# Attention scores in 64-row halves of the array: queries split on 128 rows, three passes for each head

## The chip, the cores and the metric

The kernel runs on one core of a Trainium2 chip. The metric is the device time in microseconds from the first to the last instruction on that core. The kernel before takes 1592.31 us (median of three runs, 1591.7 to 1594.3).

## What is computed

The reference is a two-layer encoder over 512 tokens of width 1024. Each layer norms its input, projects it, runs a state-space branch and an attention branch, projects both back, adds the residual, and then runs a gated feed-forward block. Cut to the part that matters here (16 query heads of 64 channels, 4 key heads, blocks of 128 queries that see the 128 keys before and behind):

```python
def one_block(args):
    qb, n = args
    kb = lax.dynamic_slice_in_dim(kp, start, KEY_SPAN, axis=1)
    vb = lax.dynamic_slice_in_dim(vp, start, KEY_SPAN, axis=1)
    s = jnp.einsum("bqgrd,bkgd->bgrqk", qb, kb,
                   preferred_element_type=jnp.float32) * scale + bias
    s = jnp.where(valid, s, -jnp.inf)
    m = jnp.maximum(jnp.max(s, axis=-1, keepdims=True), sink_l)
    p = jnp.exp(s - m)
    denom = jnp.sum(p, axis=-1, keepdims=True) + jnp.exp(sink_l - m)
    return jnp.einsum("bgrqk,bkgd->bqgrd", (p / denom).astype(vb.dtype), vb)
```

## The kernel before, in words

Matrices in float32 are split into a leading part and a trailing part (`hi`, `lo`, both of type fp32r), and a product is made of three matmuls, hi by hi, hi by lo and lo by hi. `mm3` (L263 to L265) issues these three for all dense projections; they write to the four PSUM banks of `dense_bank` (printed as `pd`). Each matmul is preceded by a load of its stationary operand (LDWEIGHTS, printed as PEld).

The attention of a layer lies beside dense work. `g_q` makes the query projection of a head group (4 heads), and its `done` takes the two result banks (two heads each, 64 rows a head) and makes four query tiles: ScalarE writes the scaled leading part on the head's own 64 rows (L629), VectorE the trailing part on the other 64 rows (L630). `k_done` has put the leading part of the keys on both halves of 128 rows (`kst_h`), and the trailing part likewise (`kst_l`). So one matmul of 128 rows takes leading and trailing queries against the leading keys, and a second one takes them against the trailing keys:

```python
mm(ps[:, :w], q, kst_h[:, g, it.k0 : it.k0 + w], start=True, stop=False)
mm(ps[:, :w], q, kst_l[:, g, it.k0 : it.k0 + w], start=False, stop=True)
```

`attn_scores` does this (L557, L558) for each of the four heads of an item, an item being one block of 128 queries of one group: w is 256 keys for the first and the last block of the sequence and 384 for the two between them. That is 2 layers x 4 groups x 4 blocks x 4 heads = 128 heads, 64 at each width. VectorE then adds the bias and takes the maximum (L559), which frees the head's bank. Score banks, transposes and value products share the four banks of `small_bank` (printed as `psm`). `attn_turn` transposes the softmax (L591; ScalarE copies the bank out in L593), `attn_values` multiplies by the values (L601) with the two halves of the columns of the array, 64 columns each, and `attn_push` runs values, turn and scores of three successive items in a row.

The `Side` object spreads these items between the steps of the dense projections, and a scheduler then sets the final order of the instructions on each engine from its own priorities. So where the score matmuls stand among the dense ones is read from the built program, not from the code.

Of the kernel before, what the change touches and what calls it, by code (L numbers as in the profile page):

```python
# [14 lines left out]
P = 128  # L15
L = 512
# [33 lines left out]
def encoder_kernel(  # L50
# [27 lines left out]
    def f(ap):  # L78
        return ap.bitcast(F32)
# [16 lines left out]
    def nm(s):  # L96
        uid[0] += 1
        return f"{s}_{uid[0]}"
# [4 lines left out]
    def small_bank():  # L103
        return pss.tile([P, 512], F32, tag="s", name=nm("psm"))

    # ------------------------------------------------------------------
    # weights: raw float32 units, split into a leading and a trailing part
    # ------------------------------------------------------------------
    units = []
# [13 lines left out]
    def kcols(w, kt0, nkt, c0, ncol):  # L123
        """rows kt0*128.. of w, columns c0..c0+ncol, as [p, kt, col]"""
        return w[kt0 * P : (kt0 + nkt) * P, c0 : c0 + ncol].rearrange("(k p) c -> p k c", p=P)
# [9 lines left out]

    # a unit is (key, [(kt0, nkt, col0, ncols, offset, pitch)], matrix)
    def prep_raw(n):
# [56 lines left out]

    # ------------------------------------------------------------------
    # constants
    # ------------------------------------------------------------------
    def tri(name, op, base, cm, step, src):
# [47 lines left out]
    def load_toep(g):  # L246
        """the table rows of a head group, once for each query of a block"""
        src = table[4 * g : 4 * g + 4].unsqueeze(0).broadcast_to([P, 4, 512])
        nc.gpsimd.dma_start(toep[g].rearrange("h p c -> p h c"), src)
# [8 lines left out]

    # ------------------------------------------------------------------
    # helpers  # L260
    # ------------------------------------------------------------------
    def mm3(o, lh, ll, rh, rl, start, stop):
# [14 lines left out]
    def norm_token(npool, t, wb, dst):  # L277
        """RMS norm of token tile t, transposed and split into dst = [(hi, lo)] * 2"""
        xn = npool.tile([P, D], F32, tag="xn", name=nm("xn"), bufs=4)
        ss = smp.tile([P, 2], F32, tag="ss", name=nm("ss"))  # L280
        halves = [slice(512 * b, 512 * b + 512) for b in range(2)]
        for b, cs in enumerate(halves):
            sq = xn[:, cs]
            if dst is None and b == 0:
                G.tensor_tensor(sq, x_sb[t][:, cs], wb[:, cs], ALU.mult)
                sq = npool.tile([P, 512], F32, tag="sq", name=nm("sq"), bufs=2)
            S.activation(sq, x_sb[t][:, cs], AF.Square, scale=1.0 / 32.0, accum_out=ss[:, b : b + 1])  # L287
        rs = smp.tile([P, 1], F32, tag="rs1", name=nm("rs"))
        G.tensor_scalar(rs, ss[:, 0:1], ss[:, 1:2], EPS, ALU.add, ALU.add)  # L289
        G.tensor_tensor(rs, rs, mhalf, ALU.pow)  # L290
        for b, cs in enumerate(halves):
            if dst is None:
                if b == 0:
                    S.mul(xn[:, cs], xn[:, cs], rs)
                else:
                    V.scalar_tensor_tensor(xn[:, cs], x_sb[t][:, cs], rs, wb[:, cs], ALU.mult, ALU.mult)
                nc.sync.dma_start(out[t * P : (t + 1) * P, cs], xn[:, cs])
            elif b == 0:
                V.scalar_tensor_tensor(xn[:, cs], x_sb[t][:, cs], rs, wb[:, cs], ALU.mult, ALU.mult)
            else:  # L300
                S.mul(xn[:, cs], x_sb[t][:, cs], rs)
                G.tensor_tensor(xn[:, cs], xn[:, cs], wb[:, cs], ALU.mult)
        if dst is None:
            return
        for b in range(2):
            ps = small_bank()
            pv = ps.rearrange("p (k c) -> p k c", k=4)
            for j in range(4):
                kt = 4 * b + j
                turn128(pv[:, j, :], xn[:, kt * P : (kt + 1) * P], ident)  # L310
            h, l = dst[b]
            hs, ls = h[:, :, t * P : (t + 1) * P], l[:, :, t * P : (t + 1) * P]
            S.copy(hs, pv)
            V.tensor_tensor(ls, pv, f(hs), ALU.subtract)

    def ws_part(key, j, acts, banks, w=None, sl=slice(0, L)):
        """k tiles 4j.. of two column tiles of a matrix, transposed"""
        hi, lo = w or take(key + (j,))
# [29 lines left out]
    def bc_last(ap, n):  # L348
        """[p, a] -> [p, a, n]"""
        return ap.unsqueeze(2).broadcast_to([P, ap.shape[1], n])  # L350
# [10 lines left out]

    # ------------------------------------------------------------------
    # layers
    # ------------------------------------------------------------------
    class Side:
        """steps that are traced between the dense units, in order"""

# [68 lines left out]
    for i in range(DEPTH):  # L436
        side = Side()
        with ExitStack() as mix:
            ep = mix.enter_context(pool(f"mixer_{i}", bufs=1, reuse_waits="tile"))

            def g_ws(key, acts, done):
                """two column tiles of a matrix, transposed: [128 columns, 512 tokens] each"""
                banks = [dense_bank() for _ in range(2)]
                for j in range(2):
                    ws_part(key, j, acts, banks)
                    if j == 1:
                        done(banks)
                    yield

# [1 line left out]
            v_sb = ep.tile([P, NT, 256], F32, name=nm("v"))  # L451
# [22 lines left out]
            def dt_step():  # L474
                # softplus(x) = max(x, 0) + 2 artanh(e / (2 + e)), e = exp(-|x|)
                def et(name, shape, dt=F32):
# [18 lines left out]

                # a * dt and its split, running sums and their exponentials
                adt = sp_e
# [25 lines left out]

# [1 line left out]
            mixA = []  # L525
# [18 lines left out]
            def attn_scores(it):  # L544
# [8 lines left out]
                G.tensor_copy(s4[:, :, w], sink4)  # L553
                for h in range(4):
                    ps = small_bank()
                    q = it.qst[h][:, n * P : (n + 1) * P]
                    mm(ps[:, :w], q, kst_h[:, g, it.k0 : it.k0 + w], start=True, stop=False)  # L557
                    mm(ps[:, :w], q, kst_l[:, g, it.k0 : it.k0 + w], start=False, stop=True)  # L558
                    V.tensor_tensor_reduce(  # L559
                        out=s4[:, h, :w],  # L560
                        in0=ps[:, :w],
                        in1=it.bias[h // 2][:, h % 2, it.j0 : it.j1],
                        scale=1.0,
                        scalar=sink4[:, h : h + 1],
                        op0=ALU.add,
                        op1=ALU.max,
                        accum_out=m4[:, h : h + 1],
                    )
                nm4 = smp.tile([P, 4], F32, tag="nm4", name=nm("nm4"))
# [52 lines left out]
            def g_q(g):  # L622
                def done(qb):
                    qst = []
                    for h in range(4):
                        q = ap.tile([P, L], F32R, tag="qst", name=nm("q"), bufs=8)
                        r = (h % 2) * HD
                        src = qb[h // 2][r : r + HD, :]
                        S.mul(q[r : r + HD], src, HD ** -0.5)  # L629
                        V.scalar_tensor_tensor(  # L630
                            q[HD - r : 2 * HD - r], src, HD ** -0.5, f(q[r : r + HD]), ALU.mult, ALU.subtract
                        )
                        qst.append(q)
                    mixA.append(stream_tile().rearrange("p (k c) -> p k c", k=2))
# [32 lines left out]

# [1 line left out]
            def g_xbc(g, r):  # L669
# [84 lines left out]
            def ssd_steps(sp, g, r):  # L754
                """the SSD of one group as a list of steps"""
                h0 = GH * g
# [10 lines left out]

                # states that enter each chunk, from before it and from behind it
                prev = [{}, {}]
# [148 lines left out]

# [1 line left out]
            x_sb = load_x(x_in if i == 0 else x_dram)  # L920
# [24 lines left out]
        def token_outer(key, nkt, acts, after):  # L945
            """[tokens, 1024] += acts.T @ w, the last two k tiles with the tokens outside"""
            banks = [(dense_bank(), small_bank()) for _ in range(NT)]
# [24 lines left out]
        with ExitStack() as ffn:  # L972
# [9 lines left out]

# [1 line left out]
            p_sb = []  # L984
# [50 lines left out]
def _onehot():  # L1035
    """relative-position bucket of column m (key - query = m - 255), as a one-hot matrix"""
    import numpy as np
# [31 lines left out]
```

## Time and profile before

| what | value |
| --- | --- |
| median of three runs | 1592.31 us (1591.7 to 1594.3) |
| profiled execution | 1591.7 us, all of it span |
| TensorE busy | 1545.5 us, 97% of the span |
| VectorE busy | 907.1 us, 57% |
| ScalarE busy | 777.5 us, 49% |
| GpSimd busy | 252.0 us, 16% |
| chain that ended last | PE 85%, DVE 8%, ACT 3% |

The profiled execution is as long as the fastest of the three runs, and 0.6 us under their median. The busy share of TensorE counts modelled ends of matmuls; how far apart two matmuls start says more about what one costs, and is read from the timeline.

### The profile page before, as it was taken

What the parts mean: (1) busy time and instruction counts of PE and PEld (TensorE: products, weight loads), DVE (VectorE), ACT (ScalarE), POOL (GpSimd) and SP (SyncE); (2) the same over time, 40 slices, a digit from 0 to 9 for tenths busy, and PEclk for the clock granted to TensorE, in tenths of its full rate; (3) what the DMA queues carried; (4) which work ended last, traced back from release to release, by engine and by line L of the source; (5) the groups of instructions that cost most, each with busy time, mean ns of one, the idle gap of its engine ahead of it and who ended that gap; (6) DMA issues with size and microseconds to landing.
All of it is one profiled execution on the core that took longest, in us unless ns stands there. A gap on an engine that the chain in (4) does not pass through costs nothing.

```text
span 1591.7 us, 20384 instructions
## 1 busy us (share of the span) xinstructions
PE 1545.5 (97%) x7796; PEld 1264.4 (79%) x7796; DVE 907.1 (57%) x1430; ACT 777.5 (49%) x1374; POOL 252.0 (16%) x320
## 2 busy tenths in 40 slices
PE   5999999999999999999999999998999999999998
PEld 5877876877888888888888788677788888888886
DVE  3667759967554444433366685797855444443333
ACT  4487886553443333322356779856435333332223
POOL 4000015546100000000020000444632000000002
PEclk9999999899999999999999999999999999999999
DMA  8423211232133223222342322113222333223221
GB/s 252 125 73 87 74 54 41 67 107 81 64 106 106 93 93 104 95 93 93 96 152 80 93 66 63 52 42 118 65 94 66 106 96 102 93 93 103 96 93 66
DMA packets 109125, 145.09 MB, mean 91 GB/s; under 512 B 7467, under 2 KB 89643, under 8 KB 109021
## 3 DMA queue, kind: packets, MB, share of 16 engines
q1 hardware_dynamic: 105476, 133.12, 26.7%
q0 software_dynamic: 2976, 10.59, 2.1%
q8 instruction: 61, 1.00, 0.3%
q14 instruction: 36, 0.29, 0.1%
q10 hardware_dynamic: 576, 0.10, 0.0%
HBM read 139.56 MB, written 8.42 MB: 93 GB/s over the span
## 4 chain that ended last, share of the span: by engine, by line
PE 85%; DVE 8%; ACT 3%; POOL 2%; issue 1%; DMA 1%; SPq 0%; POOLq 0%; ACTq 0%; DVEq 0%
PE pd L263 21%; PE pd L264 21%; PE pd L265 21%; PE psm L265 3%; PE psm L264 3%; PE psm L263 3%; PE psm L601 2%; PE psm L591 2%; DVE wlo L156 2%; DVE dd L816 1%; PE psm L557 1%; PE psm L839 1%; PE psm L826 1%; PE psm L856 1%; PE psm L558 1%
## 5 line engine op out<-in xcount | busy, mean ns | idle before, releaser
L156 DVE TENSOR_TENSOR wlo<-raw,whi 128x1024 fp32r<-128x1024 f32 (+1 forms) x230 | 285.1, 1243 | 293.8 <-ACT whi L155 293.2
L263 PE MATMUL pd<-t,whi 128*128 128x512 f32 (+1 forms) x1088 | 419.4, 386 | 0.0
L265 PE MATMUL pd<-t,wlo 128*128 128x512 f32 (+1 forms) x1088 | 417.8, 384 | 0.4 <-DVE wlo L156 0.4
L264 PE MATMUL pd<-t,whi 128*128 128x512 f32 (+1 forms) x1088 | 417.7, 384 | 0.0
L155 ACT CAST whi<-raw 128x1024 fp32r<-128x1024 f32 (+1 forms) x230 | 238.5, 1041 | 272.6 <-PE pd L264 205.0
L265 PEld LDWEIGHTS pd<-t,wlo 128*128 128x128 f32 x1088 | 204.4, 188 | 41.8 <-DVE wlo L156 1.6
L263 PEld LDWEIGHTS pd<-t,whi 128*128 128x128 f32 x1088 | 204.2, 188 | 39.9 <-issue 1.7
L264 PEld LDWEIGHTS pd<-t,whi 128*128 128x128 f32 x1088 | 204.5, 188 | 39.4 <-issue 1.0
L263 PE MATMUL pd<-whi,t 128*128 128x256 f32 (+2 forms) x544 | 187.0, 344 | 2.7 <-ACT t L749 2.6
L264 PE MATMUL pd<-wlo,t 128*128 128x256 f32 (+2 forms) x544 | 181.6, 334 | 0.1
L265 PE MATMUL pd<-whi,t 128*128 128x256 f32 (+2 forms) x544 | 181.3, 334 | 0.0
L263 PEld LDWEIGHTS pd<-whi,t 128*128 128x128 f32 x544 | 104.5, 192 | 15.0 <-ACT t L749 3.5
L264 PEld LDWEIGHTS pd<-wlo,t 128*128 128x128 f32 x544 | 104.5, 192 | 12.5 <-issue 3.4
L265 PEld LDWEIGHTS pd<-whi,t 128*128 128x128 f32 x544 | 104.1, 192 | 9.7 <-issue 1.0
L1011 ACT CAST ph<-t 128x512 fp32r<-128x512 f32 x40 | 24.8, 620 | 147.7 <-PE psm L264 137.2
L1012 DVE TENSOR_TENSOR pl<-t,ph 128x512 fp32r<-128x512 f32 x40 | 27.7, 692 | 119.4 <-ACT ph L1011 119.4
L559 DVE CUSTOM_DVE_ANT_0 s<-psm,bias,sink_all 128x256 f32<-128x256 f32 (+1 forms) x128 | 66.1, 546 | 30.4 <-PE psm L558 18.3
L360 DVE SCALAR_TENSOR_TENSOR sg<-pd,fprm,sg 128x511 f32<-128x511 f32 x88 | 65.8, 748 | 30.7 <-ACT sg L354 29.0
L573 ACT ACTIVATE s<-s,nm 128x257 f32<-128x257 f32 (+1 forms) x128 | 70.7, 554 | 15.0 <-DVE nm L570 14.7
L289 POOL TENSOR_SCALAR rs<-ss 128x1 f32<-128x1 f32 x20 | 6.0, 300 | 434.2 <-ACT xn L287 434.1
L816 DVE SCALAR_TENSOR_TENSOR dd<-cbb,dts,dd 128x128 f32<-128x128 f32 x128 | 71.2, 602 | 2.7 <-ACT dd L815 2.7
L263 PE MATMUL pd<-whi,ph 128*128 128x512 f32 x176 | 69.7, 396 | 0.0
(185 smaller groups left out, 2360.3 us busy)
## 6 DMA issues: line engine op xcount, KB each, us to landing
raw<-in_w_up_dram SPq DMA_DIRECT2D x88, 512.0 KB, 3.5
raw<-in_w_in_dram SPq DMA_DIRECT2D x52, 512.0 KB, 3.8
raw<-in_w_down_dram SPq DMA_DIRECT2D x44, 512.0 KB, 3.4
raw<-in_w_out_dram SPq DMA_DIRECT2D x32, 512.0 KB, 3.5
bias<-toep POOLq DMA_DIRECT2D x16, 384.0 KB, 4.2
raw<-in_w_in_dram SPq DMA_DIRECT2D x18, 256.0 KB, 3.4
toep<-table POOLq DMA_DIRECT2D x4, 1024.0 KB, 8.7
x<-in_x_dram SPq DMA_DIRECT2D x8, 256.0 KB, 4.6
```

Of the source, the lines that this page charges most:

```text
L155: S.copy(hi[:, :used], raw[:, :used])
L156: V.tensor_tensor(lo[:, :used], raw[:, :used], f(hi[:, :used]), ALU.subtract)
L263: mm(o, lh, rh, start=start, stop=False)
L264: mm(o, lh, rl, start=False, stop=False)
L265: mm(o, ll, rh, start=False, stop=stop)
L360: V.scalar_tensor_tensor(dst[:, lo:hi], src[:, lo + d : hi + d], taps[k], dst[:, lo:hi], ALU.mult, ALU.add)
L559: V.tensor_tensor_reduce(out=s4[:, h, :w], in0=ps[:, :w], in1=it.bias[h // 2][:, h % 2, it.j0 : it.j1], scale=1.0, scalar=sink4[:, h : h + 1],
L573: S.activation(s4[:, h, : w + 1], s4[:, h, : w + 1], AF.Exp, bias=nm4[:, h : h + 1], accum_out=den[:, h : h + 1])
L591: turn128(ps[:, c : c + P], it.s4[:, h, b * P : (b + 1) * P], ident)
L601: mm(po[c * HD : (c + 1) * HD, :256], v_sb[:, it.k0 // P + b, it.g * HD : (it.g + 1) * HD], it.pts[b][:, c * 256 : (c + 1) * 256], start=( ...
L816: V.scalar_tensor_tensor(dd[:, hs], cbb[:, cs], dts[:, c, 16 + hh + h : 17 + hh + h], dd[:, hs], ALU.mult, ALU.add)
L1012: V.tensor_tensor(l, p_sb[kt], f(h), ALU.subtract)
```

## The change

The queries are no longer stacked by part. `done` makes two tiles for each result bank, the leading part of both heads on 128 rows and the trailing part of both heads on 128 rows: two instructions on ScalarE and two on VectorE for a group in place of four and four. `attn_scores` goes by pairs of heads. A pair takes two banks at once, and three passes (leading by leading, trailing by leading, leading by trailing); in each pass the even head uses rows 0 to 63 of the array and the odd head rows 64 to 127. The product of the two trailing parts is left out. A pair so has six matmuls of 64 rows where it had four of 128 rows; in all there are 384 in place of 256. Blank lines take the place of comments elsewhere.

```diff
@@ attn_scores
-                for h in range(4):
-                    ps = small_bank()
-                    q = it.qst[h][:, n * P : (n + 1) * P]
-                    mm(ps[:, :w], q, kst_h[:, g, it.k0 : it.k0 + w], start=True, stop=False)
-                    mm(ps[:, :w], q, kst_l[:, g, it.k0 : it.k0 + w], start=False, stop=True)
-                    V.tensor_tensor_reduce(
...
+                qs, ks = slice(n * P, (n + 1) * P), slice(it.k0, it.k0 + w)
+                for pair in range(2):
+                    qh, ql = it.qst[pair]
+                    banks = [small_bank() for _ in range(2)]
+
+                    for k, (q, kst) in enumerate(((qh, kst_h), (ql, kst_h), (qh, kst_l))):
+                        for e in range(2):
+                            r = slice(e * HD, (e + 1) * HD)
+                            mm(banks[e][:, :w], q[r, qs], kst[r, g, ks], start=k == 0, stop=k == 2)
+                    for e in range(2):
+                        h = 2 * pair + e
+                        V.tensor_tensor_reduce(
...
@@ g_q, done
-                    for h in range(4):
-                        q = ap.tile([P, L], F32R, tag="qst", name=nm("q"), bufs=8)
-                        r = (h % 2) * HD
-                        src = qb[h // 2][r : r + HD, :]
-                        S.mul(q[r : r + HD], src, HD ** -0.5)
-                        V.scalar_tensor_tensor(
-                            q[HD - r : 2 * HD - r], src, HD ** -0.5, f(q[r : r + HD]), ALU.mult, ALU.subtract
-                        )
-                        qst.append(q)
+                    for src in qb:
+                        qh = ap.tile([P, L], F32R, tag="qst", name=nm("qh"), bufs=8)
+                        ql = ap.tile([P, L], F32R, tag="qst", name=nm("ql"), bufs=8)
+                        S.mul(qh, src, HD ** -0.5)
+                        V.scalar_tensor_tensor(ql, src, HD ** -0.5, f(qh), ALU.mult, ALU.subtract)
+                        qst.append((qh, ql))
```

In the changed program the score matmuls are L562, the query parts L634 and L635, the transposes L597 and the value products L607.

The first place is on TensorE, the third item of the second head group of the first layer, width 384, just behind a turn. Names: `t_67_506` are the leading keys, `t_68_507` the trailing keys. Before:

```order
L591 MATMUL psm_1204<-ident,s_177_1027 128x128 x4
L557 MATMUL psm_1214<-t_67_506,q_760 128x384
L558 MATMUL psm_1214<-t_68_507,q_760 128x384
L557 MATMUL psm_1218<-t_67_506,q_763 128x384
L558 MATMUL psm_1218<-t_68_507,q_763 128x384
L557 MATMUL psm_1222<-t_67_506,q_766 128x384
L558 MATMUL psm_1222<-t_68_507,q_766 128x384
```

The same place in the changed program:

```order
L597 MATMUL psm_1212<-ident,s_177_1031 128x128 x4
L562 MATMUL psm_1222<-t_67_506,qh_760 128x384
L562 MATMUL psm_1223<-t_67_506,qh_760 128x384
L562 MATMUL psm_1222<-t_67_506,ql_761 128x384
L562 MATMUL psm_1223<-t_67_506,ql_761 128x384
L562 MATMUL psm_1222<-t_68_507,qh_760 128x384
L562 MATMUL psm_1223<-t_68_507,qh_760 128x384
L562 MATMUL psm_1232<-t_67_506,qh_764 128x384
```

Here the two heads of a pair (banks psm_1222 and psm_1223) alternate, as the code has it, and the first pair's six matmuls are followed by the second pair's.

The second place is on TensorE too, the last item of the third head group of the first layer, width 256, among dense projections. Before:

```order
L557 MATMUL psm_1768<-t_67_506,q_920 128x256
L558 MATMUL psm_1768<-t_68_507,q_920 128x256
L264 MATMUL pd_1935<-wlo_1597,t_9_116 128x256
L265 MATMUL pd_1935<-whi_1596,t_10_117 128x256
L557 MATMUL psm_1772<-t_67_506,q_923 128x256
L558 MATMUL psm_1772<-t_68_507,q_923 128x256
L263 MATMUL pd_1935<-whi_1678,t_11_118 128x256
L264 MATMUL pd_1935<-wlo_1679,t_11_118 128x256
L557 MATMUL psm_1776<-t_67_506,q_926 128x256
L558 MATMUL psm_1776<-t_68_507,q_926 128x256
```

The same item in the changed program:

```order
L562 MATMUL psm_1796<-t_67_506,qh_924 128x256
L562 MATMUL psm_1796<-t_67_506,ql_925 128x256
L562 MATMUL psm_1796<-t_68_507,qh_924 128x256
L263 MATMUL pd_1844<-whi_1706,t_11_118 128x256
L562 MATMUL psm_1797<-t_67_506,qh_924 128x256
L562 MATMUL psm_1797<-t_67_506,ql_925 128x256
L562 MATMUL psm_1797<-t_68_507,qh_924 128x256
L264 MATMUL pd_1844<-wlo_1707,t_11_118 128x256
L562 MATMUL psm_1806<-t_67_506,qh_928 128x256
L562 MATMUL psm_1806<-t_67_506,ql_929 128x256
L562 MATMUL psm_1806<-t_68_507,qh_928 128x256
```

Here the scheduler has put the three passes of the even head (psm_1796) together, and those of the odd head (psm_1797) behind a dense matmul; the second pair follows in the same way.

The third place is on VectorE, the first query tiles and the first scores of the first layer. Before:

```order
L630 SCALAR_TENSOR_TENSOR q_648<-pd_586,q_648 64x512
L156 TENSOR_TENSOR wlo_731<-raw_622,whi_730 128x1024
L630 SCALAR_TENSOR_TENSOR q_651<-pd_586,q_651 64x512
L630 SCALAR_TENSOR_TENSOR q_654<-pd_587,q_654 64x512
L559 ISA s_98_699,m_97_698<-psm_701,bias_661,sink_all 128x256
L559 ISA m_97_698 128x1
L559 ISA s_98_699,m_97_698<-psm_705,bias_661,sink_all 128x256
L559 ISA m_97_698 128x1
```

The same place in the changed program:

```order
L635 SCALAR_TENSOR_TENSOR ql_649<-pd_586,qh_648 128x512
L156 TENSOR_TENSOR wlo_731<-raw_622,whi_730 128x1024
L635 SCALAR_TENSOR_TENSOR ql_653<-pd_587,qh_652 128x512
L565 ISA s_98_695,m_97_694<-psm_697,bias_657,sink_all 128x256
L565 ISA m_97_694 128x1
L565 ISA s_98_695,m_97_694<-psm_698,bias_657,sink_all 128x256
```

One instruction on 128 rows stands for two on 64 rows, and the same holds on ScalarE; the reductions (L565, before L559) are as many as before and come in the same order of heads.

## Rows read from the trace of the kernel before

**Rows 1.** The profile page: the span, and busy time of each engine.

```profile
span 1591.7 us, 20384 instructions
PE 1545.5 (97%) x7796; PEld 1264.4 (79%) x7796; DVE 907.1 (57%) x1430; ACT 777.5 (49%) x1374; POOL 252.0 (16%) x320
```

**Rows 2.** Attention stretches, busy us: PE, PEld, DVE, ACT, POOL; then PEclk and DMA.

```profile
68.00:222.00 154.00, 153.63 (x956) 126.35 (x955) 103.99 (x262) 124.10 (x266) 10.74 (x25) 1.00 0.26 71
848.00:1002.00 154.00, 153.57 (x945) 126.35 (x944) 102.51 (x258) 121.78 (x261) 9.90 (x25) 1.00 0.27 74
```

**Rows 3.** Groups by line and shape, score matmuls: busy us, mean ns of one.

```profile
L557 PE MATMUL psm<-t,q 128*128 128x384 f32 x64 | 24.3, 379 | 0.3 <-DVE m L559 0.2
...
L558 PE MATMUL psm<-t,q 128*128 128x384 f32 x64 | 21.6, 338 | 0.0
...
L557 PE MATMUL psm<-t,q 128*128 128x256 f32 x64 | 20.0, 321 | 0.5 <-ACT x L608 0.5
...
L558 PE MATMUL psm<-t,q 128*128 128x256 f32 x64 | 17.5, 280 | 0.0
```

**Rows 4.** Timeline of TensorE (start us, duration us): score matmuls of both widths.

```profile
851.76 0.28 PE L557 MATMUL psm<-t,q 128*128 128x256 f32 x1
851.88 0.28 PE L558 MATMUL psm<-t,q 128*128 128x256 f32 x1
...
858.32 0.34 PE L557 MATMUL psm<-t,q 128*128 128x384 f32 x1
858.49 0.34 PE L558 MATMUL psm<-t,q 128*128 128x384 f32 x1
```

**Rows 5.** Timeline, TensorE: a score run that waited, loads (PEld) and matmuls (PE).

```profile
110.78 0.19 PEld L557 LDWEIGHTS psm<-t,q 128*128 128x128 f32 x1 [0.27 <-DVE m L559]
110.78 0.44 PE L557 MATMUL psm<-t,q 128*128 128x384 f32 x1
110.89 0.19 PEld L558 LDWEIGHTS psm<-t,q 128*128 128x128 f32 x1
111.06 0.34 PE L558 MATMUL psm<-t,q 128*128 128x384 f32 x1
111.06 0.19 PEld L264 LDWEIGHTS pd<-t,whi 128*128 128x128 f32 x1
...
111.23 0.40 PE L264 MATMUL pd<-t,whi 128*128 128x512 f32 x1
```

**Rows 6.** Timeline, TensorE: value products in 64-column halves, and the way out.

```profile
93.53 0.44 PE L601 MATMUL psm<-pt,v 128*64 128x256 f32 x2
...
93.79 0.39 PE L601 MATMUL psm<-pt,v 128*64 128x256 f32 x2
...
94.22 0.39 PE L601 MATMUL psm<-pt,v 128*64 128x256 f32 x2
94.54 0.33 PE L591 MATMUL psm<-ident,s 128*128 128x128 f32 x1
```

**Rows 7.** Timeline, TensorE: from dense matmuls into 22 transposes of 8 rows and out.

```profile
63.48 0.39 PE L265 MATMUL pd<-t,wlo 128*128 128x512 f32 x1
63.80 0.22 PE L256 MATMUL psm<-ident,frow 8*128 8x8 f32 x1
...
65.12 0.20 PE L256 MATMUL psm<-ident,frow 8*128 8x8 f32 x1
65.25 0.50 PE L263 MATMUL pd<-t,whi 128*128 128x512 f32 x1
...
65.59 0.40 PE L264 MATMUL pd<-t,whi 128*128 128x512 f32 x1
65.82 0.40 PE L265 MATMUL pd<-t,wlo 128*128 128x512 f32 x1
```

**Rows 8.** Groups by line and shape, ScalarE and VectorE: the query parts.

```profile
L629 ACT ACTIVATE q<-pd 64x512 fp32r<-64x512 f32 x32 | 19.0, 593 | 13.7 <-DVE q L630 11.6 <-PE pd L265 1.8
...
L630 DVE SCALAR_TENSOR_TENSOR q<-pd,q 64x512 fp32r<-64x512 f32 x32 | 22.0, 688 | 5.6 <-ACT q L629 4.6
```

More of the change, by code (lines that the diff above doesn't have):

```diff
@@ L553, in attn_scores @@
                 G.tensor_copy(s4[:, :, w], sink4)
-                for h in range(4):
-                    ps = small_bank()
-                    q = it.qst[h][:, n * P : (n + 1) * P]
-                    mm(ps[:, :w], q, kst_h[:, g, it.k0 : it.k0 + w], start=True, stop=False)
-                    mm(ps[:, :w], q, kst_l[:, g, it.k0 : it.k0 + w], start=False, stop=True)
-                    V.tensor_tensor_reduce(
[L560 to L567, printed above, removed]
-                    )
+                qs, ks = slice(n * P, (n + 1) * P), slice(it.k0, it.k0 + w)
[9 more added lines that the diff above has]
+                        V.tensor_tensor_reduce(
+                            out=s4[:, h, :w],
+                            in0=banks[e][:, :w],
+                            in1=it.bias[pair][:, e, it.j0 : it.j1],
+                            scale=1.0,
+                            scalar=sink4[:, h : h + 1],
+                            op0=ALU.add,
+                            op1=ALU.max,
+                            accum_out=m4[:, h : h + 1],
+                        )
                 nm4 = smp.tile([P, 4], F32, tag="nm4", name=nm("nm4"))
@@ L624, in done @@
                     qst = []
-                    for h in range(4):
-                        q = ap.tile([P, L], F32R, tag="qst", name=nm("q"), bufs=8)
-                        r = (h % 2) * HD
-                        src = qb[h // 2][r : r + HD, :]
-                        S.mul(q[r : r + HD], src, HD ** -0.5)
-                        V.scalar_tensor_tensor(
-                            q[HD - r : 2 * HD - r], src, HD ** -0.5, f(q[r : r + HD]), ALU.mult, ALU.subtract
-                        )
-                        qst.append(q)
+                    for src in qb:
[4 more added lines that the diff above has]
+                        qst.append((qh, ql))
                     mixA.append(stream_tile().rearrange("p (k c) -> p k c", k=2))
```

## The prediction

> **What bounds the kernel now.** I read the page first: TensorE is busy for 1545.5 of 1591.7 us [rows 1]. Then the two stretches that hold the attention, 154 us in each layer: TensorE is busy for 153.63 and 153.57 us of them, ScalarE for some 123 and VectorE for some 103, at the full granted clock [rows 2]. So here, too, TensorE sets the pace, dense matmuls fill whatever the attention leaves free, and all that ScalarE and VectorE could give back in these stretches is 0.37 + 0.43 = 0.8 us of idle TensorE. The groups by line come next [rows 3], and last the timeline, since a matmul's duration contains a modelled end: what one costs is the distance between two starts. For a score matmul that is 0.12 us at 256 keys and 0.17 us at 384 [rows 4].
>
> **The change part by part.**
>
> *Score matmuls, streaming.* Before: 128 matmuls of each width, 128 x 0.12 + 128 x 0.17 = 37.1 us. In the changed order I counted the 64 pairs of heads. In 38 the two halves alternate as written (14 at 256 keys, 24 at 384). In 24 the scheduler has put three passes of one half behind each other (18 at 256, 6 at 384; the order section shows such an item), and 2, at 384, stand two by two. No row shows 64-row halves at work, so their price is bounded: the nearest rows are the value products in 64-column halves, where two matmuls count as one step: the pair behind 93.79 ends its modelled time as one matmul does (0.39 us for both), and two pairs take 94.22 - 93.79 = 0.43 us [rows 6]. I take that for row halves: an alternating pair costs three steps, a pair in threes six, one two by two four. That is 14 x 0.36 + 24 x 0.51 + 18 x 0.72 + 6 x 1.02 + 2 x 0.68 = 37.8 us, less 4 x 0.12 where two threes meet and overlap by one: 37.3 us. **Streaming: 0.** What alternation wins, the threes lose. The other bound is no overlap at all, 192 x 0.12 + 192 x 0.17 = 55.7 us, 18.6 more.
>
> [...]
>
> *Going into halves and out.* The nearest rows are the transposes of 8 rows between dense matmuls [rows 7]. In: 63.48 to 63.80 is 0.32, where dense matmuls stand 0.23 apart (65.59 to 65.82): 0.09. Out: the last transpose to the dense matmul takes 0.13, where 21 steps from 63.80 to 65.12 give 0.06 each: 0.07. Then that dense matmul takes 0.34 instead of 0.23: 0.11. The last is a weight load that could not be made ahead; in a score run that waited it is the same: load at 110.78, next load at 110.89, next matmul 0.28 after the first instead of 0.17 [rows 5]. A run of halves begins with such a load too, another 0.11. Together 0.09 + 0.11 + 0.07 + 0.11 = 0.38 us an excursion. The changed order has 65 unbroken runs of score matmuls, all between 128-row work but 6, which go on to the value products. 65 x 0.38 = 24.7; the six ways out that are not needed give back 6 x 0.18 = 1.1. **+23.6 us.** The bound from below is the column halves: 0.09 in, 0.05 for a first pair that takes 0.26 instead of 0.21, 0.10 out (0.32 to the transpose instead of 0.22) [rows 6], 0.24 us, or 15.6 less 0.6 = 15.0. The bound from above adds a second load in the 23 runs that begin with both halves, 23 x 0.11 = 2.5.
>
> *What of this was paid before.* The first score matmul of a head has a mean of 379 ns against 338 for the second, and 321 against 280 [rows 3]: 41 ns x 128 = 5.2 us of weight loads that waited for a bank. They are contained in the way in, now: **-5.2 us** (bound: 0, if banks are awaited as before). The value products form 32 runs instead of 36: 4 x 0.24 = **-1.0 us**.
>
> *Waits for banks.* A pair takes two of the four small banks at once, and 22 runs begin right behind transposes, which hold others until ScalarE has copied them. [...] Nearest row: a wait of 0.27 us for a bank [rows 5], so 0 to 22 x 0.27 = 5.9 us. I take 0, since the way in falls into the same time.
>
> *Query parts.* ScalarE saves 16 x 0.593 = 9.5 us and VectorE 16 x 0.688 = 11.0 us [rows 8] (64-row instructions cost by their 512 columns; I take the 128-row ones to cost the same). Both hide under a busy TensorE: 0, at most the 0.8 us above. An alternating even head is complete one step (0.12 or 0.17 us) later for VectorE's reduction, which has 50 us of slack in 154.
>
> **Sum:** 0 + 23.6 - 5.2 - 1.0 = +17.4 us on the profiled execution, 1591.7 to 1609.1. The median of the runs lies 0.6 above it: 1592.3 to **1609.7 us**. With the bounds: 15.0 - 6.2 = +8.8 (1601), and 23.6 + 2.5 + 5.9 - 1.0 = +31 at worst, of which I take half of the waits as likely: 1601 to 1618.
>
> **Rivals.**
>
> *Row halves cost nothing to enter* (faster). Nothing drains when half the rows are addressed, and loads go in turn. Then only -5.2 - 1.0 stands: 1586. It decides where an excursion costs less than 6.2 / 65 = 0.10 us. For it: the two halves of the rows are a different partition than 8 rows. Against it: both narrowings in the trace cost 0.24 or more [rows 6, 7]. Chance 0.10; a part of it ends near no change.
>
> *Loads take turns.* If the two halves cannot be loaded at once, an alternating step needs two loads of 0.11 [rows 5], 0.22 us. That adds 14 x 3 x 0.10 + 24 x 3 x 0.05 = 7.8 us: 1617.5. For it: 128 columns are loaded whatever the rows. Against it: column halves go on at 0.215 a step, though theirs are 64 columns wide [rows 6]. Chance 0.17.
>
> *The halves do not run beside each other,* so the change does not do what it says. Streaming 18.6 more: 1628. Against it: column halves do [rows 6]. Chance 0.12.
>
> *No load beside a matmul in the same half.* Then of each three behind each other two loads stand free: 48 heads x 2 x 0.11 = 10.6 us, 1620. Against it: at 111.06 a load begins with a 128-row matmul, and the next starts 0.17 us later without delay [rows 5]. Chance 0.04. [...]
>
> **How the numbers follow.** My forecast has 0.57, 1601 to 1618. The range goes from 1598, which takes in an excursion a little under the cheapest row, to 1625, which holds the turns of loads, the free loads, and the third rival where excursions are cheap: some 0.8 in all. A measurement of this kernel can tell 0.2%, 3.2 us, from no change. Faster by more: most of the first rival, 0.10. Within it: its edge and the cheapest end of mine, 0.07. Slower: 0.83.
>
> **What would show it.** In the profile after, two score matmuls of different halves start a few ns apart and the next two 0.12 or 0.17 us later (streaming); with loads in turn every step is 0.11 or more; without overlap 0.12 and 0.17 for each. The first score matmul behind a dense one starts 0.32 us after it instead of 0.23, and the dense one that follows a run is 0.34 before the next (excursions). The time lies in the two attention stretches, about 8 to 9 us longer in each. I am wrong if these steps look like those of the 128-row matmuls, if TensorE idles there for banks, or if the stretches keep their length.

## The result and the profile after

The changed kernel takes 1609.41 us (median of four runs, 1607.42 to 1611.03), against 1592.31 before: a ratio of 1.0105 over all runs, with a 95% interval from 1.0093 to 1.0117. The forecast was 1609.7 us. The profiled execution spans 1607.2 us, 15.5 more than before [rows 1], and its own time is 1608.9, so 1.7 us lie around the span.

The page, span and busy time of each engine:

```profile
span 1607.2 us, 20593 instructions
...
PE 1561.1 (97%) x7924; PEld 1264.9 (79%) x7924; DVE 886.2 (55%) x1414; ACT 758.3 (47%) x1350; POOL 251.0 (16%) x320
```

TensorE is busy 15.6 us longer, VectorE and ScalarE some 20 us less. The windows (columns as in [rows 2]) of the attention, 11 us longer than those of before, and of the first microseconds of the state-space branch (SSD below) behind it:

```profile
68.00:233.00 165.00, 163.37 (x1011) 126.68 (x1010) 97.26 (x254) 116.31 (x254) 9.28 (x24) 1.00 0.24 66
241.30:273.70 32.40, 31.63 (x141) 23.43 (x140) 31.80 (x50) 21.19 (x40) 14.99 (x17) 1.00 0.18 49
855.50:1020.50 165.00, 163.51 (x1006) 127.63 (x1005) 96.63 (x251) 115.48 (x254) 10.11 (x25) 1.00 0.25 69
```

In the attention TensorE still has work nearly all the time: 1.63 and 1.49 us idle, where it was 0.37 and 0.43 [rows 2]. The groups by line and shape of the score matmuls, which answer to [rows 3]:

```profile
L562 PE MATMUL psm<-t,qh 64*128 64x384 f32 x128 | 29.4, 375 | 0.7 <-ACT pt L599 0.7
L562 PE MATMUL psm<-t,qh 64*128 64x256 f32 x128 | 28.5, 322 | 2.4 <-DVE m L565 2.2
L562 PE MATMUL psm<-t,ql 64*128 64x384 f32 x64 | 16.0, 351 | 0.0
L562 PE MATMUL psm<-t,ql 64*128 64x256 f32 x64 | 14.7, 291 | 0.0
```

The 2.2 us at 256 keys are new: a score matmul waits for VectorE's reduction of an earlier head to free a bank. What a run of score matmuls costs stands in the timeline of TensorE (start, duration; x2 is two matmuls, in the pairs below some 0.005 us apart). First a run of twelve, in which the halves alternate:

```profile
78.70 0.39 PE L264 MATMUL pd<-t,whi 128*128 128x512 f32 x1
78.92 0.39 PE L265 MATMUL pd<-t,wlo 128*128 128x512 f32 x1
79.24 0.44 PE L562 MATMUL psm<-t,qh 64*128 64x384 f32 x2
79.52 0.34 PE L562 MATMUL psm<-t,ql 64*128 64x384 f32 x2
79.70 0.52 PE L562 MATMUL psm<-t,qh 64*128 64x384 f32 x4
80.05 0.34 PE L562 MATMUL psm<-t,ql 64*128 64x384 f32 x2
80.23 0.34 PE L562 MATMUL psm<-t,qh 64*128 64x384 f32 x2
80.50 0.50 PE L263 MATMUL pd<-t,whi 128*128 128x512 f32 x1
80.83 0.39 PE L264 MATMUL pd<-t,whi 128*128 128x512 f32 x1
```

Both halves work at once: two matmuls take one step of 0.17 to 0.18 us. The way in is 0.32 us behind a dense matmul where dense ones stand 0.22 to 0.23 apart; the first step is 0.28 instead of 0.17; the last is 0.27; and the dense matmul behind the run is 0.33 before the next. So an excursion costs 0.09 + 0.105 + 0.09 + 0.105 = 0.39 us. Then a head whose three passes stand behind each other, loads and matmuls, with dense matmuls of 256 columns behind it:

```profile
186.70 0.18 PEld L562 LDWEIGHTS psm<-t,qh 64*128 64x128 f32 x1
186.70 0.38 PE L562 MATMUL psm<-t,qh 64*128 64x256 f32 x1
186.81 0.19 PEld L562 LDWEIGHTS psm<-t,ql 64*128 64x128 f32 x1
186.92 0.28 PE L562 MATMUL psm<-t,ql 64*128 64x256 f32 x1
186.93 0.18 PEld L562 LDWEIGHTS psm<-t,qh 64*128 64x128 f32 x1
187.04 0.28 PE L562 MATMUL psm<-t,qh 64*128 64x256 f32 x1
187.24 0.19 PEld L263 LDWEIGHTS pd<-whi,t 128*128 128x128 f32 x1
187.24 0.39 PE L263 MATMUL pd<-whi,t 128*128 128x256 f32 x1
187.35 0.19 PEld L264 LDWEIGHTS pd<-wlo,t 128*128 128x128 f32 x1
187.47 0.28 PE L264 MATMUL pd<-wlo,t 128*128 128x256 f32 x1
```

One head takes 0.54 us here (186.70 to 187.24), alone on its 64 of the 128 rows. The load at 186.93 begins with the matmul at 186.92 in the same row half, and the next matmul of that half starts 0.12 later (187.04). Last, loads inside two runs of twelve that waited, at 256 and at 384 keys:

```profile
131.96 0.19 PEld L562 LDWEIGHTS psm<-t,qh 64*128 64x128 f32 x2 [0.17 <-ACT pt L599]
...
132.81 0.18 PEld L562 LDWEIGHTS psm<-t,qh 64*128 64x128 f32 x1 [0.31 <-ACT pt L599]
...
169.28 0.18 PEld L562 LDWEIGHTS psm<-t,qh 64*128 64x128 f32 x1 [0.16 <-ACT pt L599]
```

The second pair of the item waits for its two banks, which hold transposes until ScalarE (L599) has copied them; the first of these runs takes 1.40 us where one of the same width without the wait takes 0.90, the second 1.53 in place of 1.25 (starts added up from the timeline).

**Where the time went.** For each layer I took two stretches from the timeline: from the first running sum (L513) to the last value product (the attention), and from there to the first matmul of L859 (L856 before; the SSD's opening). Dense matmuls move between the stretches, so I took them off, each at the distance of two dense starts (0.228 us for 512 columns, 0.117 for 256). What is left in the attention is 80.24 and 78.90 us after, 68.01 and 68.19 before: +12.2 and +10.7. In the opening it is 12.99 against 14.63, twice: -3.3. The rest of the span makes -4.1, of which 3.9 lie in the rest of the SSD, up to the last matmul of that line: 22.9 - 3.3 - 4.1 = 15.5. So the scores cost more than the total shows, and something behind them gives 7.4 us back.

What differs there is the SSD's order on VectorE. TensorE's waits, before:

```profile
PE psm L839 <- DVE em L830: 10.5, 10, 2.9
```

and after:

```profile
PE psm L842 <- DVE em L833: 2.2, 2, 1.1
```

`em` is a product that VectorE makes for TensorE (line, us in total, times, longest). Before, its first one stands behind a row of convolution steps (L360). VectorE's timeline before:

```profile
241.87 0.74 DVE L360 SCALAR_TENSOR_TENSOR cT<-pd,cprm,cT 128x509 f32<-128x509 f32 x1
242.53 1.70 DVE L816 SCALAR_TENSOR_TENSOR dd<-cbb,dts,dd 128x128 f32<-128x128 f32 x2
244.14 1.53 DVE L830 TENSOR_TENSOR em<-em,dd 128x512 f32<-128x512 f32 x1
```

and after:

```profile
248.40 0.80 DVE L833 TENSOR_TENSOR em<-em,dd 128x512 f32<-128x512 f32 x1
249.13 0.73 DVE L360 SCALAR_TENSOR_TENSOR cT<-pd,cprm,cT 128x510 f32<-128x510 f32 x1
```

Counted from the last value product, it starts 14.02 us behind it before and 7.02 after. VectorE is the engine with the least idle time in this opening: 0.86 us before and 0.60 after, TensorE 2.39 and 0.77. Windows before, for comparison with the second row above (32.40 us, VectorE 31.80):

```profile
230.00:265.50 35.50, 33.11 (x148) 24.62 (x147) 34.64 (x52) 24.61 (x43) 15.51 (x17) 1.00 0.17 45
```

### The profile page after: what moved, and what is told of

It is laid out like the page before. It is cut to its first block, busy times and chain, and to the rows that moved or that the text cites. A ratio compares the mean times of both kernels' runs of the same rounds, so it can differ in the third digit from the quotient of the medians.

```text
span 1607.2 us, 20593 instructions
## 1 busy us (share of the span) xinstructions
PE 1561.1 (97%) x7924; PEld 1264.9 (79%) x7924; DVE 886.2 (55%) x1414; ACT 758.3 (47%) x1350; POOL 251.0 (16%) x320
## 4 chain that ended last, share of the span: by engine, by line
PE 84%; DVE 8%; ACT 2%; POOL 2%; issue 2%; DMA 1%; POOLq 0%; SPq 0%; ACTq 0%; DVEq 0%
PE pd L263 21%; PE pd L265 21%; PE pd L264 21%; PE psm L265 3%; PE psm L263 3%; PE psm L264 3%; PE psm L562 3%; PE psm L607 2%; PE psm L597 2%; DVE dd L819 2%; DVE wlo L156 2%; PE psm L829 1%; DVE xT L360 1%; PE psm L842 1%; PE psm L784 1%
## 5 line engine op out<-in xcount | busy, mean ns | idle before, releaser
L565 DVE CUSTOM_DVE_ANT_0 s<-psm,bias,sink_all 128x256 f32<-128x256 f32 (+1 forms) x128 | 65.4, 547 | 39.4 <-PE psm L562 34.3
L360 DVE SCALAR_TENSOR_TENSOR sg<-pd,fprm,sg 128x511 f32<-128x511 f32 x88 | 65.8, 748 | 30.7 <-ACT sg L354 29.0
```

The lines of the kernel that those rows point to most:

```text
L360: V.scalar_tensor_tensor(dst[:, lo:hi], src[:, lo + d : hi + d], taps[k], dst[:, lo:hi], ALU.mult, ALU.add)
L565: V.tensor_tensor_reduce(out=s4[:, h, :w], in0=banks[e][:, :w], in1=it.bias[pair][:, e, it.j0 : it.j1], scale=1.0, scalar=sink4[:, h : h + 1],
```

## The experiments

The kernel before was run again beside them, at 1592.2 to 1592.5 us. The table gives the split of each by the same working (changes in us against the profiled execution of before; "em" is how far the first decay product stands behind the last value product):

| kernel | median us | attention, two layers | opening | rest | em |
| --- | --- | --- | --- | --- | --- |
| the change | 1609.41 | +12.2, +10.7 | -3.3 | -4.1 | 7.02 |
| x1_threes | 1609.20 | +11.9, +12.0 | -4.1 | -4.9 | 7.02 |
| x4_before_half | 1615.26 | +11.7, +10.7 | 0.0 | -0.8 | 14.02 |
| x5_behind_values | 1608.61 | +11.9, +12.0 | -3.3 | -5.3 | 11.56 |
| x6_before_behind_values | 1586.69 | +1.2, +1.0 | -3.2 | -5.7 | 11.56 |
| x7_query_tiles_only | 1584.29 | -0.8, -1.1 | -4.6 | -1.5 | 8.12 |
| x8_three_full_passes | 1603.40 | +9.7, +8.5 | -4.2 | -6.5 | 6.93 |
| y1_four_evictions | 1614.24 | +16.7, +12.7 | -3.2 | -5.6 | 7.02 |
| y2_tiles_four_evictions | 1584.01 | -0.4, -0.8 | -4.6 | -4.2 | 8.12 |

**Three passes behind each other everywhere (x1_threes).**

```diff
-for k, (q, kst) in enumerate(((qh, kst_h), (ql, kst_h), (qh, kst_l))):
-    for e in range(2):
+for e in range(2):
+    for k, (q, kst) in enumerate(((qh, kst_h), (ql, kst_h), (qh, kst_l))):
```

> The changed kernel with the two loops swapped, so that no pair alternates by design: 61 runs of score matmuls instead of 65, and the two halves meet only where one head's three passes follow another's, some 67 times. My theory (a step of two halves costs one, an excursion from 128-row work 0.38 us): 67 overlaps of 0.15 us in place of the 37.3 us of streaming make 55.7 - 9.8 = 45.9, +8.6, four excursions fewer -1.5, so 1609.4 + 7 = 1616.5 us. Rival 'the halves win nothing by alternating, or what is lost lies elsewhere': 1608 to 1610. Rival 'two banks at once make the time': faster than the change, since here a head needs one bank before it starts, 1600 to 1606.

Measured: 1609.20 us, ratio 1.0109 (1.0092 to 1.0126). The loss did not come. Timeline of TensorE, a run of twelve, issued as qh, ql, qh of the even head and then of the odd head:

```profile
112.43 0.49 PE L597 MATMUL psm<-ident,s 128*128 128x128 f32 x3
112.85 0.45 PE L562 MATMUL psm<-t,qh 64*128 64x384 f32 x2
113.13 0.35 PE L562 MATMUL psm<-t,ql 64*128 64x384 f32 x2
113.31 0.78 PE L562 MATMUL psm<-t,qh 64*128 64x384 f32 x4
```

Two `qh` matmuls start together, then two `ql`: the odd head's first matmul runs beside the even head's first although two others were issued between. The steps of this pair, 0.28 and 0.18 us, are those of the run at 79.24 in the change, so here the issue order of the halves made no difference. The last four matmuls of the run start one by one (113.66, 113.83, 113.92, 114.11). Where dense work splits a pair in the change, its heads follow each other: the passes of one begin at 185.84, a dense matmul at 186.39, and the passes of the other at 186.70.

**Pairs, then items, held together (x2_pairs_held, x3_item_held).** To keep dense matmuls out, the matmuls of a pair, then of an item, were put into one section that the scheduler may not break.

```diff
+with tc.tile_critical():
     for k, (q, kst) in enumerate(((qh, kst_h), (ql, kst_h), (qh, kst_l))):
         for e in range(2):
```

> The changed kernel with the six matmuls of a pair held together, so that all 64 pairs alternate, in 64 runs of six. My theory: streaming falls from 37.3 to 27.9 us, the excursions stay (64 instead of 65), so 1609.4 - 9.4 - 0.4 = 1599.6 us, still slower than before. Rival 'threes are the whole loss': as fast as before or faster, 1585 to 1592. Rival 'two banks at once make the time': both banks must now be free before the first matmul, so no gain or a loss, 1609 or more.

> The changed kernel with the twelve matmuls of an item held together, behind the release of all four small banks: 32 runs of twelve, all alternating. My theory: streaming 27.9 (-9.4) and 33 excursions fewer (-12.5): 1609.4 - 21.9 = 1587.5 us, faster than before by 0.3%. Rival 'banks make the time': four banks at once starve TensorE, 1600 or more.

Measured: 1754.72 us (1.1018, 1.1001 to 1.1034) and 1710.21 us (1.0747, 1.0724 to 1.0770). Both expectations missed, and both runs tell nothing of the array: the section brings waits of its own. TensorE's waits in x2_pairs_held:

```profile
PE psm L563 <- DMA raw<-in_w_in_dram: 36.9, 15, 3.3
PE psm L563 <- issue: 24.0, 20, 4.2
```

A score matmul has no use for the weights that arrive by that DMA.

**The old scores on 64 rows (x4_before_half).** Two passes, no overlap to gain, 78 runs.

```diff
-mm(ps[:, :w], q, kst_h[:, g, it.k0 : it.k0 + w], start=True, stop=False)
-mm(ps[:, :w], q, kst_l[:, g, it.k0 : it.k0 + w], start=False, stop=True)
+r = slice(0, HD)
+mm(ps[:, :w], q[r], kst_h[r, g, it.k0 : it.k0 + w], start=True, stop=False)
+mm(ps[:, :w], q[r], kst_l[r, g, it.k0 : it.k0 + w], start=False, stop=True)
```

> The kernel before, with both score passes of every head on rows 0 to 63 only (it leaves out the products of the other 64 rows): as many score matmuls of the same widths, one bank at a time, no alternation, the old query tiles; only the excursions are added, 78 of them. My theory: 78 x 0.38 = 29.6 less 5.2 of loads that were paid before, so 1592.3 + 24.4 = 1616.7 us. Rival 'entering half of the rows costs little, the loss is the third pass or the banks': 1592 to 1596.

Measured: 1615.26 us, ratio 1.0145 (1.0129 to 1.0160). The number of matmuls, their columns and the order of the SSD's steps are those of before, so the +22.4 us in the attention are the price of going into half the rows and out, where 24.4 were expected. Timeline of TensorE, between dense matmuls:

```profile
185.74 0.28 PE L263 MATMUL pd<-whi,t 128*128 128x256 f32 x1
185.99 0.38 PE L558 MATMUL psm<-t,q 64*128 64x256 f32 x1
186.21 0.27 PE L559 MATMUL psm<-t,q 64*128 64x256 f32 x1
186.41 0.38 PE L264 MATMUL pd<-wlo,t 128*128 128x256 f32 x1
186.63 0.28 PE L265 MATMUL pd<-whi,t 128*128 128x256 f32 x1
```

The steps are 0.25, 0.22, 0.20 and 0.22 us where each would be 0.12 on the whole array: 0.41 us over four.

**A third pass on all 128 rows (x8_three_full_passes).** The kernel before with its first score matmul of each head issued twice.

```diff
 mm(ps[:, :w], q, kst_h[:, g, it.k0 : it.k0 + w], start=True, stop=False)
+mm(ps[:, :w], q, kst_h[:, g, it.k0 : it.k0 + w], start=False, stop=False)
```

> The kernel before with the first score matmul issued twice (it counts the leading keys' product twice): 384 matmuls of 128 rows, no halves, no excursion. My theory: a third pass costs its streaming, 64 x 0.12 + 64 x 0.17 = 18.9 us: 1611 us, as slow as the change, with all of it in the score matmuls and none in the dense ones behind them. Rival 'TensorE has room in the attention stretches': under 1600.

Measured: 1603.40 us, ratio 1.0066 (1.0051 to 1.0081). The theory's 1611 missed. In the attention the third pass costs 18.2 us, close to the 18.6 of 128 more matmuls at 0.12 and 0.17 [rows 4], but the rest of the span gives 10.7 back (in the profiled execution, the fastest of the four, which range from 1600.9 to 1605.0). So 384 matmuls of 128 rows cost 4.7 us less there than the change's 384 of 64 rows, although by the prediction's working the steps of the change make 37.3 us and those of 384 matmuls of 128 rows 55.7.

**The query tiles alone (x7_query_tiles_only).** The change's tiles, scores in two passes of 128 rows.

```diff
-mm(ps[:, :w], q, kst_h[:, g, it.k0 : it.k0 + w], start=True, stop=False)
-mm(ps[:, :w], q, kst_l[:, g, it.k0 : it.k0 + w], start=False, stop=True)
+mm(ps[:, :w], qh[:, qs], kst_h[:, g, ks], start=True, stop=False)
+mm(ps[:, :w], ql[:, qs], kst_l[:, g, ks], start=False, stop=True)
```

> The changed kernel's query tiles alone (two instructions on ScalarE and two on VectorE for a group), with two 128-row score matmuls for each head as before (they multiply both heads of a pair at once, leading by leading and trailing by trailing, so each score is that sum). My theory: the saved 9.5 us of ScalarE and 11 us of VectorE hide under TensorE, 1592 within 1.5 us. Rival 'the lighter evictions gave back the 7 us that the changed kernel regains behind the attention': 1584 to 1588.

Measured: 1584.29 us, ratio 0.9946 (0.9930 to 0.9963): 8 us less than my theory, and inside the range of its rival. Either the cheaper query parts are worth it, as the rival has it, or the order of instructions is. The next four tell these apart.

**The query parts in four and four instructions again (y1 to y4).** In the changed kernel (y1) and in x7 (y2):

```diff
-S.mul(qh, src, HD ** -0.5)
-V.scalar_tensor_tensor(ql, src, HD ** -0.5, f(qh), ALU.mult, ALU.subtract)
+for r in (slice(0, HD), slice(HD, P)):
+    S.mul(qh[r], src[r], HD ** -0.5)
+    V.scalar_tensor_tensor(ql[r], src[r], HD ** -0.5, f(qh[r]), ALU.mult, ALU.subtract)
```

> The changed kernel, but each query tile is written by two instructions of 64 rows on ScalarE and two on VectorE, four and four for a group as before the change; the score matmuls are the change's own. In the built order they form 77 unbroken runs where the change has 65. Theory: the cheaper query parts were worth some 8 us, and an excursion costs 0.39 us; so 1609.4 + 8 + 12 x 0.39 = 1622 us. Rival (the query parts are hidden, as the prediction said, and the 8 us of the run that had only the query tiles came from another order of instructions): 1609.4 + 4.7 = 1614 us. Rival (neither matters): 1609.4.

> The kernel that has only the change's query tiles (128-row score matmuls in two passes, sums over both heads, so that the products mix the heads; 1584.3 us), but each tile written by two instructions of 64 rows on ScalarE and two on VectorE. Layout and passes are those of the 1584.3 us kernel, the eviction's instructions are as many as in the kernel before. Theory (the time of the evictions carries the gain): 1592.3 us, within 1.5. Rival (the gain comes from the order or the layout): 1584.3, within 1.5.

> As the run before it, but ScalarE writes each leading tile with one instruction of 128 rows, and VectorE the trailing one with two of 64 rows. If ScalarE's part of the evictions carries the gain: 1584.3 us; if VectorE's does: 1592.3; if both take part: about 1588. If the gain is the order's and not the time's, this one lands anywhere from 1584 to 1592 and the next does not complement it.

> The complement: ScalarE writes each leading tile with two instructions of 64 rows, VectorE the trailing one with one of 128 rows. If VectorE's part carries the gain: 1584.3 us; if ScalarE's does: 1592.3; if both take part: about 1588, and its gain and that of the run before add up to 8 us.

Measured: y1 1614.24 us (1.0137, 1.0121 to 1.0154), y2 1584.01 (0.9947, 0.9932 to 0.9961), y3 1586.42 (0.9964, 0.9951 to 0.9977), y4 1585.22 (0.9956, 0.9941 to 0.9971). My theory fell, and with it the rival that x7 had seemed to confirm: with the old number of evictions the gain is still there (y2), and merging them on both engines, one or none gives 1584.3, 1586.4, 1585.2 and 1584.0 us, with no sense in it. The evictions' time is hidden, and y1 is the change plus 12 excursions: 4.8 us by the medians (6.5 in the attention alone), where 12 x 0.39 = 4.7 were expected. The gain of x7 and y2 lies in the SSD for the most part (6.1 of 8.0 us, and 8.8 of 10.0, by the spans), where `em` stands 8.12 us behind the values in place of 14.02.

**Scores behind the values (x5_behind_values on the changed kernel, x6_before_behind_values on the one before).** The score step goes between the values and the turn; x5 also swaps the two loops, as x1 does, and pins the order of its score matmuls.

```diff
 attn_values(line[k - LAG - 2])
-if k >= LAG + 1 and line[k - LAG - 1]:
-    attn_turn(line[k - LAG - 1])
 if it:
     attn_scores(it)
+if k >= LAG + 1 and line[k - LAG - 1]:
+    attn_turn(line[k - LAG - 1])
```

> The changed kernel with the scores of an item issued between the value products and the turn of the older items, and each score matmul pinned behind the one before it in the program (three passes of one half, then of the other): 39 runs of score matmuls instead of 65, 27 of them with all twelve of an item, and 26 that begin straight behind value products in column halves, so that one way out serves both. My theory: an excursion is 0.40 us apart and 0.20 behind value products, 10.4 us instead of 24.8; the halves overlap wherever both stand in one run, 30.0 us of streaming instead of 36.5; the value products now form 48 runs instead of 32, +4.8; in all 1609.4 - 16.1 = 1593.3 us. Rival 'waiting for banks makes the time': the banks are wanted right behind each other as before, 1605 or more.

> The kernel before with the same new place of the scores, between value products and turn, and its 128-row score matmuls unchanged: the control for the run above. My theory: 128-row scores enter and leave nothing, so the place matters only through the value products' runs, 1592 within 2 us. Rival 'the place itself saves waits': under 1588.

Measured: x5 1608.61 us (1.0102, 1.0087 to 1.0117), x6 1586.69 (0.9963, 0.9950 to 0.9976). x5 has 39 runs of score matmuls in place of 65, and its attention is no shorter. TensorE's waits in x5_behind_values:

```profile
PE psm L598 <- DVE m L566: 9.2, 13, 2.1
...
PE psm L562 <- DVE m L566: 3.5, 9, 0.9
```

The transposes now stand right behind the scores and wait for VectorE's reductions to free their banks. That is 12.7 us of waits for reductions where the change has 2.2. Each distance between two starts in the attention can be given to the earlier of the two matmuls; a dense one gets its usual distance, and what is over goes to the work beside it. Counted so, and without the 5.5 us for which the transposes right behind them wait, the score matmuls of x5 take 17.2 us less than those of the change; the transposes with that wait take 12.0 more, and the value products, in 48 runs in place of 32, 6.1 more. So fewer excursions did pay, and other work took it back. x6 computes what before and the change compute, and beats both, which my theory for it missed. Its attention is 2.2 us longer than before, so the place saves nothing there; what it gains lies behind the attention.

## Why the prediction was right, and where only its sum was

*Streaming, taken as 0: right.* Alternating pairs take three steps of 0.17 or 0.12 us, and a head in threes three steps of its own. The second rival, loads in turn, is out: both halves together pay one exposed load of 0.105 us at the start of a run, and none later. The third, no overlap, is out by the rows at 79.24 and 79.52, and the fourth, no load beside a matmul in the same half, by those at 186.92 and 186.93.

*Excursions, 0.38 us each: right.* 0.39 by the rows, with 0.09 for the way out in place of 0.07. The first rival, free entry, is out. x4 carries the price without any overlap (22.4 of the 24.4 us expected), y1 twelve more of them. The two exposed loads, 0.105 us each, are more than half of the cost; what the 0.09 us on either side consist of is not shown.

*Waits for banks, taken as 0: the step that failed in the attention.* I took both ends for hidden and let the way in cover them. At the entry of the runs that held: beyond the way in, and the load behind the run before, the timeline has 3.2 us of waits there, in four runs among dense matmuls and none in the 22 behind transposes that I had priced, and 3.5 in the kernel before. What I had not priced stands inside the runs of twelve, where the second pair waits for its two banks: eight at 384 keys take 1.52 us in place of 1.25, four at 256 take 1.40 in place of 0.90, some 4 us. That is within the 5.9 us that I gave as the bound, but at another place. One of my signs of being wrong did show: TensorE idles 2.3 us longer in the two stretches. The 5.2 us that I took off as paid before hold: the score runs of before take 44.2 us where their columns take 37.1, and 1.7 of the difference are the ends of transposes (a run of before starts 0.03 us behind the last transpose, one of the change 0.20). Counted by the distances between starts, as for x5, the attention's +22.9 us are +20.6 in the score matmuls, +2.8 in the transposes with the ways in behind them, -1.0 in the value products and +0.5 in the rest. So the scores cost 23.4 us more, where the terms of the prediction for them make 18.4; the waits inside the runs are most of the difference.

*Value products, -1.0: right,* 42.3 us before and 41.3 after by the same working.

*Query parts, taken as 0: right,* by y2 against x7 and by y1. That 128 rows cost what 64 do holds too: one takes 602 ns on ScalarE (L634) and 684 on VectorE (L635), where one on 64 rows took 593 and 688. x7 alone had looked like the opposite.

*The time lies in the attention, 8 to 9 us a layer: wrong.* The attention grew by 12.2 and 10.7 us, and the SSD behind it gave back 7.4. That the sum came out right is luck: an underestimate of 5.5 us and a gain that I had not foreseen nearly cancel, 17.4 forecast, 15.5 measured between the spans. The last part is the profiled execution of before: 1.7 us lie around a span, as the result above shows, so it was some 1 us above its median and not 0.6 below. Two slips in the working leave the forecast as it is: the steps of the streaming add up to 37.7 us and not 37.8, and the upper end with half of the waits is 1620 and not 1618.

*What stays open.* In before and in x4 the first `em` stands 14.02 us behind the last value product, and x4 keeps the time of before outside the attention within 0.8 us. In the eight other kernels of the table it stands 6.9 to 11.6 us behind, and they gain 6.1 to 10.7 us outside the attention. The two go together in ten kernels; the place of `em` was not moved alone, so it is not shown that this order is the cause. Three stretches of before have a granted clock of 0.50 or 0.51 of full speed (from 276.30, 307.00 and 1102.40 us, 3.4, 6.8 and 3.4 us long). The windows view of the longest, and of the stretch of the same length ahead of it:

```profile
300.20:307.00 6.80, 4.72 (x40) 4.51 (x38) 5.61 (x7) 3.20 (x8) 6.32 (x7) 1.00 0.27 77
...
307.00:313.80 6.80, 6.00 (x22) 4.97 (x23) 5.79 (x12) 4.16 (x10) 1.61 (x2) 0.50 0.23 74
```

TensorE was busy for 4.72 of the 6.80 us before the clock fell. The change has one such stretch, of 3.4 us (0.50, from 1118.40 us), beside the one at the program's end. Apart from the program's end, all of them lie in the SSD behind its opening, so the clock has no part in the opening's 3.3 us. Behind the opening, the second layers can be compared, with one stretch of 3.4 us in either kernel (windows from the first to the last matmul of L856 before, of L859 after):

```profile
1045.60:1174.00 128.40, 120.76 (x644) 98.43 (x643) 103.28 (x143) 65.20 (x123) 68.35 (x69) 0.99 0.22 74
...
1060.50:1189.50 129.00, 122.42 (x653) 100.30 (x652) 102.11 (x144) 66.33 (x124) 69.02 (x69) 0.99 0.22 74
```

The change does nine dense matmuls more there; without them, at 0.228 us, it is 1.5 us shorter at the same mean clock of 0.99. In the first layer, where before has 10.2 us at a clock of 0.50 and the change none, it is 2.5 us shorter. So the clock's part in the 7.4 us is some 1 us by this estimate, and most of the gain is there without it. A run of alternating pairs alone, without waits, was not had.

## What to carry to other kernels

Before a matmul is split into row halves, count the unbroken runs that the built order leaves, and price each with a way in, a way out and a weight load at both ends: here 65 runs of 0.39 us cost more than a third pass over the whole array would (the change 1609.41 us, x8 1603.40). Count the waits inside a run as well as at its start: a pair takes two banks at once, and the second pair of an item waited in the middle of the run (1.40 us at 256 keys where 0.90 do without the wait). And when a scheduler sets the order, compare the stages behind the change too: an edit to the scores moved VectorE's queue in another branch (its first `em` from 14.02 to 7.02 us behind the last value product), and a control that undoes the cost in question (y2) tells such a gain from the edit's own.

## What was not expected of the hardware

A matmul of the other row half, three places later in the issue order, started with the first: the row at 112.85 in x1_threes holds both and lasts 0.45 us, where one alone lasts 0.44 (207.51 in the change). The loads of both halves go side by side: the first step of a run at 384 keys is 0.28 us for two matmuls (at 79.24) and also for one (at 207.51), against 0.17 to 0.18 later. And a chain of three matmuls in one half at 256 keys takes 0.12 us from the second to the third (186.92 to 187.04), the step of the whole array [rows 4], with the load at 186.93 beside the matmul ahead of it.
